# Up-projection by Strassen's seven products on 258-token blocks, its activations through DRAM

## The chip, the core and the metric

The kernel runs on one core of a Trainium2 chip. The metric is device time in microseconds, and lower is better; a run is the time of one launch. TensorE (PE in the profile) multiplies, VectorE (DVE), ScalarE (ACT) and GpSimd (POOL) do the elementwise work, and SyncE (SP) issues the transfers between DRAM and the on-chip memory (SBUF). Products land in PSUM, which TensorE writes and the other engines read.

## The reference

One layer of a hybrid decoder trunk on 1024 prompt tokens and 8 sample tokens (NT = 1032 columns), 1024 features, all float32. The part that the change touches is the MLP with what stands directly ahead of it and behind it:

```python
x = x + concat([o, sg]) @ w_out                                              # 1024 x 1024
x = x + square(relu(rms_norm(x, g_ff) @ w_up)) @ w_down                      # w_up 1024 x 4096, w_down 4096 x 1024
x = x + (p @ w_ple) * sigmoid(rms_norm(x, g_ple) @ w_ple_gate)
y = rms_norm(x, g_final)
```

Ahead of it lie the input projection, a gated delta rule with four heads, and a causal spatial gate.

## The kernel before

Activations lie feature-major: a tile is 128 features by 1032 tokens. A float32 product is made of three TensorE passes: each operand is split into a rounded half (hi, type fp32r) and the rest (lo), and `gemm_steps` issues hi·hi, lo·hi and hi·lo (lines 164 to 166) into one PSUM block. The tokens go in three blocks of 384, 384 and 264 columns, so that one weight tile of 128 x 128 is loaded for each matmul. Weights come in as tiles `st` of 512 KB; ACT rounds them (`whi`, line 133) and DVE subtracts (`wlo`, line 136).

The program is laid out in stages. From 0 to about 521 us the input projection and the two mixing branches are woven together on TensorE. Then the second half of the out-projection runs (`out_half(1)`, about 522 to 567 us): `evo` adds each block to the residual `X1[m]` on DVE (line 1003) and, in the same place, `split_gain` gives the scaled halves `XN[m]` that the MLP reads (lines 139 and 140). The rms factor needn't be known then: the squares' sum `ss` is built on ACT and POOL (lines 1081 to 1086) beside the first MLP products, and since relu squared is homogeneous, the reciprocal mean square `rr` is multiplied into the down-projection's results (`evd`, line 1151).

The MLP runs in eight groups. A group has four up units (128 hidden features each, eight feature tiles deep), whose evacuation `evu` applies relu and square on ACT and makes the halves of h (lines 1137 to 1140) in the tiles RA[8..15], and then four down units that read these h tiles at once and add to `X1` (DVE line 1151, POOL line 1153; in the last group DVE does the add and `split_gain` for the next stage). The hidden activations never leave SBUF. Weights are taken in the order of the list `plan` by `next_w`: `stage` issues the next tile's transfer on SP (line 1050) and `halves` splits it, one unit ahead. TensorE's order is that of the code; the other engines' order is set by a scheduler that takes instructions with high priority (evacuations, weight halves) first. The engines go through their queues strictly in order, and so does SP, where a transfer that waits holds up those behind it.

Behind the MLP stands the gate stage, which neither kernel makes differently.

Of the kernel before, what the change touches and what calls it, by code (L numbers as in the profile page):

```python
# [8 lines left out]
F32 = mybir.dt.float32  # L9
# [7 lines left out]
P = 128  # L17
# [51 lines left out]
def trunk_step_kernel(  # L69
# [49 lines left out]
    dram = ctx.enter_context(pool("dram", 1, DRAM))

# [4 lines left out]

    RA = [act.tile([P, NT], F32R, name=f"ra{i}") for i in range(16)]
# [15 lines left out]
    def load_w(src, hi_eng=S, lo_eng=V, prio=PRI):  # L142
        """src: [128, k, m] view in DRAM, k * m = 1024."""
        a, b = src.shape[1], src.shape[2]
        st = wst.tile([P, 1024], F32, tag="st", name="st")
        hi = wsp.tile([P, 1024], F32R, tag="whi", name="whi")
        lo = wsp.tile([P, 1024], F32R, tag="wlo", name="wlo")
        with tc.high_priority(prio):
            SY.dma_start(st.rearrange("p (a b) -> p a b", a=a), src)
            split(hi[:, :], lo[:, :], st[:, :], hi_eng, lo_eng)  # L150
        return hi.rearrange("p (a b) -> p a b", a=a), lo.rearrange("p (a b) -> p a b", a=a)

    gps = [None]
# [36 lines left out]
    def weave(main):  # L190
        """Put in main's products; between them, what the tasks have ready by then: a task yields
# [1122 lines left out]
```

## Time and profile before

| | us |
|---|---|
| median of three runs | 1438.74 (1437.06 to 1439.82) |
| span of the profiled execution | 1437.0 |
| TensorE matmuls busy | 1383.8 (96%) |
| VectorE busy | 731.3 (51%) |
| ScalarE busy | 499.0 (35%) |
| GpSimd busy | 496.2 (35%) |

The profiled execution shows its span alone; no separate run time of that same execution is given. The span is read as the length of one launch on the core, and the median of the runs lies 1.7 us above it. Busy shares are averages over all stages. Matmuls are shown pipelined: the duration of one is longer than the distance to the next, so costs of TensorE are taken from the distance between starts.

### The profile page before, as it was taken

The numbers are of one execution on the slowest core, as the hardware profiler recorded it, in microseconds if no ns is written. First come the engines' busy times: TensorE is split into PE (matmuls) and PEld (weight loads), VectorE is DVE, ScalarE is ACT, GpSimd is POOL, SyncE is SP. The second block draws the span as 40 slices with busy tenths as digits, with TensorE's granted clock in tenths as the row PEclk, the third lists the DMA queues.
The fourth block names the chain that finished last, engine by engine and source line by source line (L and its number), as shares of the span: only waits on it lengthen the run. The fifth ranks groups of instructions, "written<-read, shape, count | busy, mean of one in ns | idle before, by whom it ended". The sixth has DMA issues, their size and how long they took to land.

```text
span 1437.0 us, 22992 instructions
## 1 busy us (share of the span) xinstructions
PE 1383.8 (96%) x9087; PEld 1358.1 (95%) x9087; DVE 731.3 (51%) x1452; ACT 499.0 (35%) x1056; POOL 496.2 (35%) x590
## 2 busy tenths in 40 slices
PE   6999978999998999999999999999999999998998
PEld 4999977999898999999999999999999999998998
DVE  7746655368847656333433333434333333496336
ACT  6576546432234235312203122131121311344345
POOL 5301987847416215042140321403214032053331
PEclk8999988999999999999999999999999999999999
DMA  7335536465438531111111111111111111111224
GB/s 232 97 87 154 142 78 156 152 177 154 119 83 237 198 120 45 60 44 45 45 46 58 44 45 45 45 48 56 45 45 45 45 48 56 45 44 45 60 59 162
DMA packets 169095, 126.11 MB, mean 88 GB/s; under 512 B 15937, under 2 KB 156428, under 8 KB 168981
## 3 DMA queue, kind: packets, MB, share of 16 engines
q1 hardware_dynamic: 168988, 124.66, 29.0%
q8 instruction: 71, 1.16, 0.3%
q14 instruction: 36, 0.29, 0.1%
HBM read 97.94 MB, written 26.80 MB: 87 GB/s over the span
## 4 chain that ended last, share of the span: by engine, by line
PE 77%; DVE 10%; POOL 4%; ACT 3%; DMA 3%; issue 2%; SPq 0%; DVEq 0%; ACTq 0%; POOLq 0%
PE g L164 23%; PE g L165 23%; PE g L166 23%; POOL xinv L594 2%; POOL it L593 2%; DVE wlo L136 1%; DVE x L1153 1%; DVE ra L136 1%; PE mx L924 1%; PE em L1192 1%; PE em L1191 1%; PE g L376 1%; PE em L1193 1%; DVE ra L140 1%; DVE rlt L211 1%
## 5 line engine op out<-in xcount | busy, mean ns | idle before, releaser
L164 PE MATMUL g<-ra,whi 128*128 128x384 f32 (+1 forms) x2016 | 667.4, 331 | 1.9 <-DVE t L1151 1.0
L165 PE MATMUL g<-ra,wlo 128*128 128x384 f32 (+1 forms) x2016 | 651.7, 323 | 1.3 <-DVE wlo L136 1.3
L166 PE MATMUL g<-ra,whi 128*128 128x384 f32 (+1 forms) x2016 | 650.6, 323 | 0.6 <-POOL ra L341 0.4
L164 PEld LDWEIGHTS g<-ra,whi 128*128 128x128 f32 x2016 | 384.5, 191 | 4.6 <-DVE t L1151 1.3
L165 PEld LDWEIGHTS g<-ra,wlo 128*128 128x128 f32 x2016 | 384.6, 191 | 2.0 <-DVE wlo L136 1.6
L166 PEld LDWEIGHTS g<-ra,whi 128*128 128x128 f32 x2016 | 383.8, 190 | 2.5 <-POOL ra L341 1.3
L1153 POOL TENSOR_TENSOR x<-x,t 128x384 f32<-128x384 f32 x168 | 155.7, 927 | 479.4 <-DVE t L1151 479.0
L133 ACT CAST whi<-st 128x1024 fp32r<-128x1024 f32 x112 | 117.1, 1046 | 311.2 <-PE g L166 309.3
L1151 DVE TENSOR_TENSOR t<-g,rr 128x384 f32<-128x384 f32 (+1 forms) x192 | 98.6, 513 | 177.4 <-PE g L166 177.4
L136 DVE TENSOR_TENSOR wlo<-st,whi 128x1024 fp32r<-128x1024 f32 x111 | 142.0, 1279 | 53.6 <-ACT whi L133 53.6
L164 PE MATMUL g<-rb,whi 128*128 128x384 f32 (+1 forms) x480 | 154.6, 322 | 0.0
L1139 DVE TENSOR_TENSOR q<-t 128x384 f32<-128x384 f32 (+1 forms) x96 | 49.6, 517 | 204.0 <-ACT t L1137 204.0
L166 PE MATMUL g<-rb,whi 128*128 128x384 f32 (+1 forms) x480 | 153.4, 320 | 0.0
L165 PE MATMUL g<-rb,wlo 128*128 128x384 f32 (+1 forms) x480 | 153.2, 319 | 0.0
L1137 ACT ACTIVATE t<-g 128x384 f32<-128x384 f32 (+1 forms) x96 | 44.0, 458 | 248.7 <-PE g L166 248.7
L1086 POOL TENSOR_TENSOR ss<-ss,q 128x384 f32<-128x384 f32 (+1 forms) x62 | 67.3, 1093 | 167.0 <-ACT q L1085 167.0
L593 POOL TENSOR_TENSOR it<-ainv,xinv 32x31 f32<-32x31 f32 (+15 forms) x124 | 76.1, 614 | 44.5 <-DMA ainv<-inv_d 35.1
L166 PEld LDWEIGHTS g<-rb,whi 128*128 128x128 f32 x480 | 90.6, 189 | 0.0
L165 PEld LDWEIGHTS g<-rb,wlo 128*128 128x128 f32 x480 | 90.5, 189 | 0.0
L164 PEld LDWEIGHTS g<-rb,whi 128*128 128x128 f32 x480 | 90.4, 188 | 0.1
L594 POOL TENSOR_TENSOR xinv<-xinv,it 32x31 f32<-32x31 f32 (+15 forms) x124 | 81.1, 654 | 9.6
L1140 DVE TENSOR_TENSOR ra<-q,ra 128x384 fp32r<-128x384 f32 (+1 forms) x96 | 49.4, 515 | 7.0 <-DVE q L1139 0.5
(339 smaller groups left out, 1374.7 us busy)
## 6 DMA issues: line engine op xcount, KB each, us to landing
st<-in_w_up SPq DMA_DIRECT2D x32, 512.0 KB
st<-in_w_down SPq DMA_DIRECT2D x32, 512.0 KB
st<-in_w_in SPq DMA_DIRECT2D x24, 512.0 KB
ck<-ck_d SPq DMA_DIRECT2D x32, 320.0 KB
st<-in_w_ple_gate SPq DMA_DIRECT2D x16, 512.0 KB
x<-xfm_d SPq DMA_DIRECT2D x8, 516.0 KB
xt<-in_x_prompt SPq DMA_DIRECT2D x8, 512.0 KB
s<-in_state_gdn SPq DMA_DIRECT2D x8, 512.0 KB
```

The source lines that it names most:

```text
L133: S.copy(dst_hi, src)
L136: lo_eng.tensor_sub(dst_lo, src, f32(dst_hi))
L164: PE.matmul(ps[:, :w], lhsT=whi[k], rhs=xh, start=(k == 0), stop=False)
L165: PE.matmul(ps[:, :w], lhsT=wlo[k], rhs=xh, start=False, stop=False)
L166: PE.matmul(ps[:, :w], lhsT=whi[k], rhs=xl, start=False, stop=(k == nk - 1))
L593: G.tensor_mul(tv, a, x)
L594: G.tensor_sub(X[:, j + 1 :, :w], X[:, j + 1 :, :w], tv)
L1086: G.tensor_add(ss[:, b], ss[:, b], q[:, :w])
L1139: V.tensor_mul(q[:, :w], t[:, :w], t[:, :w])
L1140: V.tensor_sub(lo[:, o : o + w], q[:, :w], f32(hi[:, o : o + w]))
L1151: V.tensor_mul(t[:, :w], ps[:, :w], rr[:, o : o + w])
L1153: (V if b == 7 else G).tensor_add(xv, xv, t[:, :w])
```

## The change

The MLP is taken apart into two stages. The up-projection is computed by Strassen's scheme in Winograd's form: the 1024 input features are halved into k = 0..3 and k = 4..7 and the 256 output features of a pair of units into two; the input block's and the weight block's quarters are combined by sums, seven products take the place of eight, and sums of the products give the outputs. The tokens are cut into four blocks of 258, and a product multiplies one combination on 258 columns: two token halves t, each with an even and an odd block, are the input's second dimension of the scheme.

For this, the input needs seven combinations per token half, in halves hi and lo. `xform(k, tp)` makes them as soon as `out_half(1)` has finished the feature tiles k and k + 4 on a token half: two ACT scalings (line 1058), three POOL subtractions (lines 1060 to 1062), one ACT rounding (line 1066) and one DVE subtraction (line 1067) of 7 x 258 columns. All eight calls work in one buffer `Q` and write to `FB`, 14 cells of 2064 columns. `up_forms` loads the four quarters of the weights for a pair of units, forms four sums on POOL (lines 1134, 1137, 1140, 1145) and splits seven forms; three forms are kept ahead. `up_stage` runs 16 pairs of 7 products with 2 token halves, 4 feature tiles and 3 passes each on 258 columns, in the PSUM banks A, C, D and E. `hidden` applies relu and square on ACT, a square on POOL and a subtraction on DVE, and stores hi and lo of h to DRAM, `h_d` (line 1201), from two buffers `hs`. The statistics for `rr` are made by `up_rows` beside it (line 1212 is its add on POOL).

The down-projection follows as a separate stage with the blocks and units of before: it loads h from `h_d` into cells of `FB` that the last products have released (`load_h`, line 1296), three groups of four ahead. Its first weight tile lies in a pool `wst2` that takes the space of the up stage's tiles, the second in the older pool `wst`. Weights are split in two forms of 512 columns each instead of one of 1024, everywhere. The core of the diff:

```diff
+HB = NT // 4
+QBLK = [(i * HB, HB) for i in range(4)]
+STEPS = (("P1", 0, "A", True, False), ("P5", 3, "D", True, False), ("P6", 5, "A", False, True), ("P7", 4, "C", True, False),
+         ("P2", 2, "E", True, True), ("P4", 6, "C", False, True), ("P3", 1, "D", False, True))
+FREE = [x[1] for x in STEPS]
+AHEAD = 3
...
-    wsp = ctx.enter_context(pool("wsp", 2))
...
+    wst = ctx.enter_context(pool("wst", 1, side="right"))
+    wsp = ctx.enter_context(pool("wsp", 4, side="right"))
...
+    def form(src, hi_eng=S, lo_eng=V):
+        hi = wsp.tile([P, 512], F32R, tag="whi", name="whi").rearrange("p (a b) -> p a b", a=4)
+        lo = wsp.tile([P, 512], F32R, tag="wlo", name="wlo").rearrange("p (a b) -> p a b", a=4)
+        split(hi, lo, src, hi_eng, lo_eng)
+        return hi, lo
...
+    h_d = dram.tile([32, P, 2, NT], F32, name="h_d")
...
-            RB = [sr.tile([P, NT], F32R, tag=t, bufs=b, name="rb")
-                  for t, b in (("at", 2), ("at", 2), ("sf", 2), ("sf", 2), ("dt", 1), ("kp", 1), ("kt", 1), ("vt", 1))]
-            XN = [(RA[2 * m], RA[2 * m + 1]) if m < 4 else (RB[2 * m - 8], RB[2 * m - 7]) for m in range(KD)]
...
+                sizes = QBLK if half else BLK
...
-                            if half:
-                                split_gain((XN[m][0][:, b], XN[m][1][:, b]), X1[m][:, b], gff[:, m : m + 1])
...
+                    if half == 0:
+                        for j in range(2):
+                            yield from steps(j, range(NB))
+                    else:
+                        for tp in range(2):
+                            for j in range(2):
+                                yield from steps(j, (2 * tp, 2 * tp + 1))
+                            done(m, tp)
...
+            fst = ctx.enter_context(pool("fst"))
+            FB = fst.tile([P, 14, 8 * HB], F32R, name="fb")
+            Q = fst.tile([P, 8, HB], F32, name="q8")
+            def xform(k, tp):
+                t0 = 2 * HB * tp
+                for i in range(2):
+                    S.activation(Q[:, 2 * i : 2 * i + 2, :].rearrange("p a b -> p (a b)"), X1[k + 4 * i][:, t0 : t0 + 2 * HB],
+                                 AF.Copy, scale=gff[:, k + 4 * i : k + 4 * i + 1])
+                G.tensor_sub(Q[:, 4:6, :], Q[:, 0:1, :].to_broadcast([P, 2, HB]), Q[:, 1:3, :])
+                G.tensor_sub(Q[:, 6, :], Q[:, 2, :], Q[:, 4, :])
+                G.tensor_sub(Q[:, 7, :], Q[:, 3, :], Q[:, 6, :])
+                cells = FB[:, 7 * tp : 7 * tp + 7, :]
+                hi = cells[:, :, HB * k : HB * k + HB]
+                lo = cells[:, :, HB * (k + 4) : HB * (k + 5)]
+                S.copy(hi, Q[:, 1:8, :])
+                V.tensor_sub(lo, Q[:, 1:8, :], f32(hi))
+            weave(out_half(1, xform))
...
-        for j in range(4):
-            hi, lo = RA[8 + 2 * j], RA[9 + 2 * j]
-
-            def evu(ps, n, o, w):
-                t = tp.tile([P, BW], F32, tag="t", name="t")
-                q = tp.tile([P, BW], F32, tag="q", name="q")
-                S.activation(t[:, :w], ps[:, :w], AF.Relu)
-                S.activation(hi[:, o : o + w], t[:, :w], AF.Square)
-                V.tensor_mul(q[:, :w], t[:, :w], t[:, :w])
-                V.tensor_sub(lo[:, o : o + w], q[:, :w], f32(hi[:, o : o + w]))
...
+    def up_forms():
+        for p in range(16):
+            with tc.high_priority(PRI):
+                ra = wst.tile([P, 2, 4, P], F32, tag="st", name="ra")
+                rb = [tp.tile([P, 4, P], F32, tag="rb", bufs=4, name="rb") for _ in range(2)]
+                for i in range(2):
+                    SY.dma_start(ra[:, i], up_quarter(2 * p, i))
+                    SY.dma_start(rb[i], up_quarter(2 * p + 1, i))
+            a11, a12 = ra[:, 0], ra[:, 1]
+            a21, a22 = rb
+            yield form(a11)
+            s1 = tp.tile([P, 4, P], F32, tag="sa", bufs=1, name="s1")
+            G.tensor_add(s1, a21, a22)
+            yield form(s1)
+            s2 = tp.tile([P, 4, P], F32, tag="sb", bufs=1, name="s2")
+            G.tensor_sub(s2, s1, a11)
+            yield form(s2)
+            s3 = tp.tile([P, 4, P], F32, tag="sa", bufs=1, name="s3")
+            G.tensor_sub(s3, a21, a11)
+            yield form(s3)
+            yield form(a12)
+            yield form(a22)
+            s4 = tp.tile([P, 4, P], F32, tag="sa", bufs=1, name="s4")
+            G.tensor_sub(s4, a12, s2)
+            yield form(s4)
...
+    def up_stage():
+        forms = up_forms()
+        ahead = [next(forms) for _ in range(AHEAD)]
+        for p in range(16):
+            bank, u1, u2, u3 = {}, {}, {}, {}
+            for name, f, b, first, last in STEPS:
+                wh, wl = ahead.pop(0)
+                w = next(forms, None)
+                if w:
+                    ahead.append(w)
+                for t in range(2):
+                    if first:
+                        bank[b, t] = pu.tile([P, 512], F32, tag=f"{'A' if b == 'E' else b}{t}", name=b)[:, :HB]
+                    ps = bank[b, t]
+                    x = FB[:, 7 * t + f, :].rearrange("p (j k c) -> p j k c", j=2, c=HB)
+                    for k in range(4):
+                        PE.matmul(ps, lhsT=wh[:, k, :], rhs=x[:, 0, k, :], start=(first and k == 0), stop=False, skip_group_check=True)
+                        PE.matmul(ps, lhsT=wl[:, k, :], rhs=x[:, 0, k, :], start=False, stop=False, skip_group_check=True)
+                        PE.matmul(ps, lhsT=wh[:, k, :], rhs=x[:, 1, k, :], start=False, stop=(k == 3), skip_group_check=True)
+                        if k < 3:
+                            yield 3 * HB * 0.000455
+                    q = Q[:, 4 * t : 4 * t + 4, :]
+                    with tc.high_priority(PRI):
+                        if name == "P1":
+                            u1[t] = tp.tile([P, HB], F32, tag="u1", name="u1")
+                            S.copy(u1[t], ps)
+                        elif name == "P6":
+                            u2[t] = tp.tile([P, HB], F32, tag="u2", name="u2")
+                            S.copy(u2[t], ps)
+                        elif name == "P7":
+                            u3[t] = tp.tile([P, HB], F32, tag="u3", name="u3")
+                            V.tensor_add(u3[t], u2[t], ps)
+                            V.tensor_add(q[:, 2], u3[t], bank["D", t])
+                        elif name == "P2":
+                            V.tensor_add(q[:, 1], u1[t], ps)
+                        elif name == "P4":
+                            V.tensor_add(q[:, 3], u2[t], ps)
+                        elif name == "P3":
+                            V.tensor_add(q[:, 0], u2[t], ps)
+                    if name == "P4":
+                        hidden(2 * p + 1, t, q[:, 2:4])
+                    elif name == "P3":
+                        hidden(2 * p, t, q[:, 0:2])
+                    yield 3 * HB * 0.000455
...
+    def hidden(u, t, q):
+        S.activation(q, q, AF.Relu)
+        hs = tp.tile([P, 2, 2 * HB], F32R, tag="hs", name="hs")
+        v = hs.rearrange("p j (a b) -> p j a b", a=2)
+        S.activation(v[:, 0], q, AF.Square)
+        G.tensor_mul(q, q, q)
+        V.tensor_sub(v[:, 1], q, f32(v[:, 0]))
+        SY.dma_start(h_d[u, :, :, 2 * HB * t : 2 * HB * t + 2 * HB], f32(hs))
...
+            ss = tp.tile([P, 264], F32, tag="sq0", bufs=1, name="ssu")
+            S.activation(ss[:, :w], X1[0][:, o : o + w], AF.Square)
+            for m in range(1, KD):
+                q = tp.tile([P, 264], F32, tag="sq1", bufs=1, name="qu")
+                S.activation(q[:, :w], X1[m][:, o : o + w], AF.Square)
+                G.tensor_add(ss[:, :w], ss[:, :w], q[:, :w])
+                yield 5.0
...
+    with tc.manual_schedule(engines={mybir.EngineType.PE}):
+        spawn(up_rows(), 10.0)
+        weave(up_stage())
+        drain()
+    ust.close()
...
+    wst2 = ctx.enter_context(pool("wst2", side="right"))
...
+    cells = [FB[:, 7 * t + f, :] for f in FREE for t in range(2)]
+    def cell(i):
+        v = cells[i].rearrange("p (j c) -> p j c", j=2)
+        return v[:, 0, :], v[:, 1, :]
...
+            st = (wst if n % 2 else wst2).tile([P, 1024], F32, tag="st", name="st")
...
+    xs = [cell((m + 8) % 12) for m in range(KD)]
+    HC = [cell(u % 12) for u in range(32)]
+    def load_h(b):
+        for u in range(4 * b, min(4 * b + 4, 32)):
+            SY.dma_start(f32(cells[u % 12]).rearrange("p (j c) -> p j c", j=2), h_d[u])
+    def down():
+        load_h(0)
+        load_h(1)
+        for b in range(8):
+            load_h(b + 2)
+            hs = HC[4 * b : 4 * b + 4]
+            for m2 in range(4):
+                ws = next_w()
...
```

On POOL, at the start of the up stage, the rows of before are the sums of squares (`ss`) and then the first adds of the down-projection's results:

```order
L1086 TENSOR_TENSOR ss_6389<-ss_6389,q_6445 128x264
L1086 TENSOR_TENSOR ss_6389<-ss_6389,q_6448 128x384
L1086 TENSOR_TENSOR ss_6389<-ss_6389,q_6451 128x384
L1086 TENSOR_TENSOR ss_6389<-ss_6389,q_6454 128x264
L1153 TENSOR_TENSOR x1_5442<-x1_5442,t_6893 128x384
L1153 TENSOR_TENSOR x1_5442<-x1_5442,t_6909 128x384
L1153 TENSOR_TENSOR x1_5442<-x1_5442,t_6925 128x264
```

On POOL of the changed kernel, at the same place, rows from the end of the fifth `xform` into the sixth (`q8` is the buffer `Q`, `s1` to `s4` the weight sums of the first pair, `ssu` the squares' sum):

```order
L1062 TENSOR_TENSOR q8_6085<-q8_6085 128x258
L1212 TENSOR_TENSOR ssu_6789<-ssu_6789,qu_6791 128x256
L1134 TENSOR_TENSOR s1_6652<-rb_6642,rb_6643 128x512
L1212 TENSOR_TENSOR ssu_6789<-ssu_6789,qu_6870 128x256
L1137 TENSOR_TENSOR s2_6658<-s1_6652,ra_6641 128x512
L1140 TENSOR_TENSOR s3_6664<-rb_6642,ra_6641 128x512
L1060 TENSOR_TENSOR q8_6085<-q8_6085 128x516
L1212 TENSOR_TENSOR ssu_6789<-ssu_6789,qu_6952 128x256
L1061 TENSOR_TENSOR q8_6085<-q8_6085 128x258
L1145 TENSOR_TENSOR s4_6762<-ra_6641,s2_6658 128x512
L1212 TENSOR_TENSOR ssu_6789<-ssu_6789,qu_7015 128x256
L1062 TENSOR_TENSOR q8_6085<-q8_6085 128x258
```

Sums of weights and of squares stand ahead of the sixth `xform`'s first subtraction and between its others.

On SP, around the first change from up to down, the rows of before:

```order
L1050 DMA st_6581<-in_w_up 128x8x128
L1117 DMA row_d_99<-row_6474 9x128
L1118 DMA rr_6390<-row_d_99 128x1032
L1050 DMA st_6680<-in_w_down 128x4x256
L1050 DMA st_6779<-in_w_down 128x4x256
L1050 DMA st_6878<-in_w_down 128x4x256
L1050 DMA st_6980<-in_w_down 128x4x256
L1050 DMA st_7082<-in_w_up 128x8x128
```

On SP of the changed kernel, around its one change from up to down (`fb` are the cells that take h, `hs` the stores of h, `st_10984` the second unit's weights and `st_10982` the first unit's):

```order
L1296 DMA fb_6084<-h_d_88 128x2064 x2
L1259 DMA st_10984<-in_w_down 128x4x256
L1296 DMA fb_6084<-h_d_88 128x2064
L1201 DMA h_d_88<-hs_10698 256x1x516
L1296 DMA fb_6084<-h_d_88 128x2064 x3
L1201 DMA h_d_88<-hs_10717 256x1x516
L1296 DMA fb_6084<-h_d_88 128x2064 x5
L1201 DMA h_d_88<-hs_10900 256x1x516
L1201 DMA h_d_88<-hs_10919 256x1x516
L1201 DMA h_d_88<-hs_10938 256x1x516
L1201 DMA h_d_88<-hs_10957 256x1x516
L1259 DMA st_10982<-in_w_down 128x4x256
```

Behind the loads of h now stand four stores and, last, the weights that the first down unit needs.

On ACT, the rows of before at the first change from up to down:

```order
L1138 ACTIVATE ra12_94<-t_6707 128x384
L1137 ACTIVATE t_6738<-g_6713 128x384
L1138 ACTIVATE ra12_94<-t_6738 128x384
L1137 ACTIVATE t_6769<-g_6744 128x264
L133 CAST whi_6775<-st_6680 128x1024
L1138 ACTIVATE ra12_94<-t_6769 128x264
L1137 ACTIVATE t_6806<-g_6781 128x384
```

On ACT of the changed kernel, at its change from up to down:

```order
L142 CAST whi_10822<-s4_10820 128x512
L1195 ACTIVATE q8_6085<-q8_6085 128x516 x3
L1198 ACTIVATE hs_10900<-q8_6085 128x516
L1195 ACTIVATE q8_6085<-q8_6085 128x516
L1198 ACTIVATE hs_10919<-q8_6085 128x516
L1198 ACTIVATE hs_10938<-q8_6085 128x516
L1198 ACTIVATE hs_10957<-q8_6085 128x516
L142 CAST whi_10986<-st_10982 128x512
L142 CAST whi_10990<-st_10982 128x512
L142 CAST whi_11008<-st_10984 128x512
```

The squares that fill the last `hs` buffers now stand ahead of the rounding of the first down weights.

## Rows read from the trace of the kernel before

**Rows 1.** The page's first rows: the span, each engine's busy time:

```profile
span 1437.0 us, 22992 instructions
...
PE 1383.8 (96%) x9087; PEld 1358.1 (95%) x9087; DVE 731.3 (51%) x1452; ACT 499.0 (35%) x1056; POOL 496.2 (35%) x590
```

**Rows 2.** Busy time by engine, 600 to 1250 us (last: granted clock, DMA share, GB/s):

```profile
core 0: us, PE busy (x) PEld busy (x) DVE busy (x) ACT busy (x) POOL busy (x), PEclk, DMA share, GB/s
...
600.00:1250.00 650.00, 650.00 (x4136) 650.00 (x4135) 246.07 (x402) 138.28 (x235) 155.73 (x168) 1.00 0.15 47
```

**Rows 3.** TensorE in order of time (start, duration, line, shape):

```profile
561.10 0.34 PE L164 MATMUL g<-ra,whi 128*128 128x384 f32 x1
...
565.30 0.28 PE L164 MATMUL g<-ra,whi 128*128 128x264 f32 x1
...
577.29 0.28 PE L164 MATMUL g<-ra,whi 128*128 128x264 f32 x1
...
578.75 0.29 PE L164 MATMUL g<-rb,whi 128*128 128x264 f32 x1
```

**Rows 4.** Groups by line and form, 505 to 600 us (count, total, mean):

```profile
L133 ACT CAST whi<-st 128x1024 fp32r<-128x1024 f32 x8 | 8.3, 1041 | 8.3 <-PE g L166 8.3
...
L139 ACT ACTIVATE ra<-x,vec 128x384 fp32r<-128x384 f32 x8 | 4.9, 617 | 8.7 <-DVE x L1003 8.7
...
L139 ACT ACTIVATE ra<-x,vec 128x264 fp32r<-128x264 f32 x4 | 2.1, 513 | 1.4 <-DVE x L1003 1.4
...
L136 DVE TENSOR_TENSOR wlo<-st,whi 128x1024 fp32r<-128x1024 f32 x8 | 9.8, 1228 | 3.2 <-ACT whi L133 3.2
```

**Rows 5.** Groups by line and form, 600 to 1250 us:

```profile
L1153 POOL TENSOR_TENSOR x<-x,t 128x384 f32<-128x384 f32 x112 | 113.6, 1014 | 457.7 <-DVE t L1151 457.7
...
L1153 POOL TENSOR_TENSOR x<-x,t 128x264 f32<-128x264 f32 x56 | 42.2, 753 | 21.7 <-DVE t L1151 21.4 <-DMA st<-in_w_up 0.3
...
L1140 DVE TENSOR_TENSOR ra<-q,ra 128x384 fp32r<-128x384 f32 x59 | 32.9, 558 | 6.5 <-DVE q L1139 0.5
L1138 ACT ACTIVATE ra<-t 128x384 fp32r<-128x384 f32 x59 | 31.0, 526 | 1.9
...
L1138 ACT ACTIVATE ra<-t 128x264 fp32r<-128x264 f32 x29 | 12.3, 425 | 0.0
...
L1140 DVE TENSOR_TENSOR ra<-q,ra 128x264 fp32r<-128x264 f32 x29 | 12.4, 427 | 0.0
```

**Rows 6.** One evacuation in order of time, ACT to DVE:

```profile
600.16 0.49 ACT L1137 ACTIVATE t<-g 128x384 f32<-128x384 f32 x1 [3.16 <-PE g L166]
...
600.69 0.56 DVE L1139 TENSOR_TENSOR q<-t 128x384 f32<-128x384 f32 x1 [2.98 <-ACT t L1137]
```

**Rows 7.** Transfers on the chain that ended last (start, us, what):

```profile
108.94 3.58 DMA at<-rb_d
...
504.13 6.03 DMA st<-in_w_ple
```

**Rows 8.** Three busy stretches of transfers, columns as in rows 2:

```profile
465.00:470.00 5.00, 4.30 (x23) 3.98 (x21) 5.00 (x4) 2.92 (x8) 4.53 (x3) 0.72 1.06 376
15.00:20.00 5.00, 2.63 (x9) 1.69 (x9) 3.56 (x9) 2.59 (x6) 1.21 (x2) 0.72 1.01 391
464.40:467.80 3.40, 3.40 (x18) 3.40 (x17) 3.40 (x6) 2.20 (x8) 2.33 (x2) 0.50 1.06 342
```

**Rows 9.** What SP waited for (total us, times, longest):

```profile
SPq L149 <- DMA st<-in_w_out: 9.7, 3, 4.7
```

**Rows 10.** TensorE behind an idle stretch (brackets: idle before, releaser):

```profile
463.58 0.49 PE L685 MATMUL cb<-st,ck 128*128 128x128 f32 x2 [3.31 <-DVE vn L674]
```

**Rows 11.** A stretch of TensorE at the gate stage, columns as in rows 2:

```profile
1304.10:1310.80 6.70, 6.53 (x26) 6.39 (x27) 4.83 (x17) 0.69 (x2) 1.13 (x2) 0.50 0.26 78
```

**Rows 12.** POOL and DVE in order of time, 456 to 460 us:

```profile
456.62 2.57 POOL L972 TENSOR_TENSOR s<-s,ub 128x1024 f32<-128x1024 f32 x1
...
457.14 2.47 DVE L136 TENSOR_TENSOR ra<-uk,ra 128x384 fp32r<-128x384 f32 x1
```

More of the change, by code (lines that the diff above doesn't have):

```diff
@@ L124, in trunk_step_kernel @@
     G.memset(ones, 1.0)
-    RA = [act.tile([P, NT], F32R, name=f"ra{i}") for i in range(16)]
     def f32(ap):
@@ L1063, in trunk_step_kernel @@
[L1063 to L1086 removed]
+                            V.tensor_add(X1[m + 4 * j][:, b], X1[m + 4 * j][:, b], ps[:, :w])
@@ L1160, in trunk_step_kernel, with up_quarter @@
-    wpl = [(x1p.tile([P, D], F32R, name=f"wpl_h{k}"), x1p.tile([P, D], F32R, name=f"wpl_l{k}")) for k in range(2)]
+    ust = ExitStack()
+    tp = ust.enter_context(pool("ut", 2, side="right"))
+    pu = ust.enter_context(pool("pu", 1, PSUM))
+    pss = ust.enter_context(pool("pssu", 2, PSUM))
+    def up_quarter(u, half):
+        return w_up[0, 512 * half : 512 * half + 512, u * P : u * P + P].rearrange("(k p) m -> p k m", p=P)
+    def up_forms():
[23 more added lines that the diff above has]
+            yield form(s4)
@@ new lines, in stage, with halves @@
+    def stage():
+        n = len(staged)
+        if n < len(plan):
+            src, by_m = plan[n]
+            st = (wst if n % 2 else wst2).tile([P, 1024], F32, tag="st", name="st")
+            v = st.rearrange("p (a b) -> p a b", a=4 if by_m else 8)
+            with tc.high_priority(PRI):
+                SY.dma_start(v, src)
+            staged.append([v[:, :, j * P : j * P + P] if by_m else v[:, 4 * j : 4 * j + 4, :] for j in range(2)])
+    def halves():
+        n = len(ready)
+        if n < len(plan):
+            with tc.high_priority(PRI):
+                ready.append([form(x) for x in staged[n]])
@@ new lines, in trunk_step_kernel, with next_w, add_ss @@
+    stage()
+    stage()
+    halves()
+    cur = [0]
+    def next_w():
+        halves()
+        stage()
+        cur[0] += 1
+        return ready[cur[0] - 1]
+    def add_ss(m, b):
+        if m == 0:
+            S.activation(ss[:, b], X1[m][:, b], AF.Square)
+        else:
+            q = tp.tile([P, BW], F32, tag="q", name="q")
+            w = b.stop - b.start
+            S.activation(q[:, :w], X1[m][:, b], AF.Square)
+            G.tensor_add(ss[:, b], ss[:, b], q[:, :w])
+    xs = [cell((m + 8) % 12) for m in range(KD)]
@@ L1161, in trunk_step_kernel @@
+    with tc.manual_schedule(engines={mybir.EngineType.PE}):
+        weave(down())
+    wpl = [[half[:, :D] for half in cell(12 + k)] for k in range(2)]
     for k in range(2):
@@ L1163, in trunk_step_kernel @@
         SY.dma_start(st, w_ple[0, k * P : (k + 1) * P, :])
-        split(wpl[k][0][:, :], wpl[k][1][:, :], st[:, :], S, V)
-    pp = [(RA[8 + 2 * k], RA[9 + 2 * k]) for k in range(2)]
+        split(wpl[k][0], wpl[k][1], st[:, :], S, V)
+    pp = [cell(4 + k) for k in range(2)]
     pt = []
```

215 lines of the change are left out of this document (92 added, 123 removed).

## The prediction

> **What bounds the kernel now.** The page first: TensorE is busy for 1383.8 of 1437.0 us, every other engine for about half or less [rows 1]. An average hides stages, so the busy times by stretch come next: from 600 to 1250 us, the MLP, matmuls fill 650.00 of 650.00 us at clock 1.00, while DVE has 246, ACT 138 and POOL 156 us [rows 2]. Nothing but fewer or shorter matmuls can shorten that stretch, and any idle TensorE there is added in full. The price of a matmul comes from distances between starts: 24 of 384 columns from 561.10 to 565.30 us, 0.175 us each, and 12 of 264 from 577.29 to 578.75, 0.1217 us [rows 3]. A line through both gives 0.119 us for 258 columns. The groups by line give the other engines' prices [rows 4, 5].
>
> **Up-projection: fewer columns.** Before, 32 units x 8 feature tiles x 3 passes = 768 sets of blocks: 1536 matmuls x 0.175 + 768 x 0.1217 = 362.3 us. After, 16 pairs x 7 products x 2 halves x 4 tiles x 3 passes = 2688 x 0.119 = 319.9 us. The gain is 42.4 us; 35.2 if 258 columns cost as much as 264, 46.2 if the price is proportional to the columns (0.1176). The down and gate stages keep their columns (0), and half 1 of the out-projection, 384 matmuls x 0.119 = 45.7 us against 45.3, costs 0.4. So the question is what the new stage borders cost; before, TensorE had work of the same kind on both sides of every unit, and [rows 2] shows no border at all.
>
> **Prices of the new elementwise work.** Each comes from two forms of the same operation, by a line. ACT square or relu on 516 columns: 0.526 at 384, 0.425 at 264, so 0.64; ACT with gain, 0.617 and 0.513, so 0.73; the rounding of 7 x 258 = 1806 columns from 1.041 at 1024 and the same slope, 1.70. DVE: 0.558 at 384, 1.228 at 1024, so 2.05 at 1806, 0.70 at 516 or 512, 0.42 at 258. POOL: 1.014 and 0.753, so 1.30 at 516, 1.29 at 512, 0.74 at 258 [rows 4, 5]. A hand-over between engines takes 0.04 us (600.16 + 0.49 to 600.69) [rows 6].
>
> **Into the up stage: +33 us.** All eight `xform` calls share one buffer, so each waits for the last one's DVE subtraction. One link: 2 x 0.73 ACT, 1.30 + 0.74 + 0.74 POOL, 1.70 ACT, 2.05 DVE and some hand-overs, 8.2 us. The first can begin when half 1 has done 48 matmuls, 5.7 us into it. Eight links end at 5.7 + 65.6 = 71.3 us, while half 1 ends at 45.7. The queue of POOL adds to it: ahead of the sixth link's first subtraction stand `s1`, `s2` and `s3`, and inside it `s4` and adds of squares. `s1` needs the quarter `rb`, whose space is let go by TensorE's last matmul of half 1, and whose transfer takes about 3.6 us (512 KB alone, 3.58 [rows 7]); so `s1` ends near 45.7 + 0.4 + 3.4 + 1.3 = 50.8, `s3` near 54, and the sixth link, due at POOL at 48.2, loses 6 us there and about 2 more inside; the adds ahead of the seventh cost 1. The eighth ends near 81. TensorE can put the first product's first tiles (some 21 matmuls, 2.5 us) ahead of the last links and then waits: 81.5 - 2.5 - 45.7 = 33 us. Ends: 23 if POOL's extra rows find room (the bare chain), 40 if DVE's long subtractions also wait for POOL (below).
>
> **Inside the up stage: 0.** Per pair TensorE needs 20.0 us. ACT has 7 roundings of 512, 8 relus and squares and 4 copies, 11 us; DVE 7 x 0.70 + 4 x 0.70 + 10 x 0.42 = 11.9; POOL 4 x 1.29 + 4 x 1.30 = 10.4, and 2.3 more while the squares' sum runs. Each is under 20. But they aren't independent: a DVE subtraction of 384 columns that takes 0.558 us elsewhere [rows 5] took 2.47 when it began beside a POOL operation, and ended just after it (456.62 + 2.57 = 459.19 against 459.61) [rows 12]. Counting DVE's eleven subtractions with two SBUF operands (7.7 us) and POOL one after the other, the pair needs 18.1 us, 20.4 with the squares: still TensorE, barely. I take 0, and keep the upper end for a rival. The Trainium skill, page "SBUF — State Buffer", section "SBUF: two separate sides", calls this an exclusive lock: of a GpSimd operation and a DVE operation with two SBUF inputs, the one that starts first keeps the pair of ports, and the other fully blocks; 0.558 against 2.47 us here agrees. By that rule, kept to operations with two SBUF inputs, the sum stays as it is.
>
> **From up to down: +32 us.** Before, weights came one tile ahead and h never left the chip. Now twelve loads of h of 1.057 MB each go out as the last pair frees cells, the first 1.4 us after that pair's start; the pair ends at 20.0. Among and behind them SP has five stores of 0.53 MB and, last, the first unit's weights. Together 12.68 + 2.64 + 0.52 = 15.85 MB. The trace's busiest stretches moved 376 and 391 GB/s at a DMA share of one [rows 8]. I take 385: 41.2 us, from 2.6 us on. SP goes in order, and an issue behind others waits, as the out-projection's weights did behind earlier transfers (up to 4.7 us) [rows 9]. The last two squares on ACT wait for `hs` buffers, thus for stores that lie in that stream (the one of `hs_10919` lands near 44.5); then square 0.64, POOL 1.30, DVE 0.70, an issue 0.4, the weights 3.6, and halves 0.63 + 0.70: 8 us. The first down matmul comes at 52.5 us, 32.5 after the last up matmul; I take 32. Ends: 20 if only the loads are ahead (12.68 MB at 391 GB/s, 35 us, and 5 behind), 44 if the rate is the lowest of the three stretches, 342 [rows 8], with two returns of 3.6 us from stores in line rather than beside the loads. The Trainium skill, page "DMA: Bandwidth & Descriptors", gives about 435 GB/s as the fabric's ceiling and about 358 for HBM with one core's share; by 435 the stall would be 27 us, by 358 it would be 36. The trace's 391 speaks against 358 as a ceiling.
>
> **The clock: +3.4 us.** After an idle of 3.31 us [rows 10] TensorE ran 3.40 us at granted clock 0.50, that is 1.2 instead of 2.4 GHz [rows 8], 1.7 us lost. Two long idles cost 2 x 1.7; a stretch of 6.7 us at 0.50 is there too, at the gate stage [rows 11], so 6.8 is the upper end.
>
> **Other edits.** Weights split in two forms cost ACT 2 x 0.63 against 1.04 and DVE 2 x 0.70 against 1.23 per tile, 0.2 us each on engines with room: 0, within 2 us over the in-projection. The down stage's loads of h, 4.2 MB per group of 45 us beside 2.1 MB of weights, need 140 GB/s: hidden, 0.
>
> **Sum.** 1437.0 - 42.4 + 0.4 + 33 + 0 + 32 + 3.4 = 1463.4 us of span; the median lies 1.7 above the profiled span, so 1465.
>
> **Rivals.**
> (a) The borders cost little: POOL's rows find room (23), and the stores and first weights pass the loads, so that only the last pair's own tail (relu, square, POOL, DVE, store, weights, halves: about 9 us) is left. 1437 - 42.4 + 0.4 + 23 + 9 + 3.4 + 1.7 = 1432, faster. It decides if the first weights land within 9 us of the last up matmul. For it: a transfer of 512 KB alone takes 3.58 us; against it: one in company took 6.03 [rows 7], and SP's order puts them last. Chance 0.08.
> (b) DVE and POOL become the up stage's bound: if all of DVE's queue stands still while POOL runs, since the operations behind a blocked one wait too, a pair needs 11.9 + 10.4 = 22.3 us, and 16 x 2.3 = 37 us come on top: 1502. For it: 2.47 us in [rows 12]; against it: ten of DVE's operations read PSUM and can run beside POOL. It decides from the point where less than 2.3 us per pair overlap. Half of it is likelier than all. Chance 0.15, a third of that beyond my range.
> (c) Only one border is at its low end and the columns are proportional (-46.2): about 1437 + 1.7 - 46.2 + 0.4 + 23 + 20 + 3.4 = 1439, no change to measure. Chance 0.04.
> That fewer columns are run is certain: the built program has 2688 matmuls of 258 columns there.
>
> **How the numbers follow.** The forecast as worked out has 0.73. Low end with both borders at their lower bounds, 1441; high end with both at their upper, the clock at 6.8 and the gain 42.4: 1437 - 42.4 + 0.4 + 40 + 44 + 6.8 + 1.7 = 1488, and 1492 with a part of (b). 0.2%, about what a measurement of this kernel can tell from no change, is 2.9 us. Faster is (a), 0.08; within 0.2% 0.04; slower 0.88.
>
> **What would show it.** In the profile after: matmuls 0.119 us apart in the up stage, 320 us of them; one idle of about 33 us ended by DVE's subtraction of 1806 columns, and one of about 32 ended by halves of `w_down`, whose transfer stands last on SP; a granted clock of 0.5 behind both; no idle between pairs. I am wrong if TensorE's idle at either border is under 10 us, or if idle lies scattered over the up stage with DVE or POOL as releaser.

## The result and the profile after

The changed kernel takes 1479.47 us (1478.17 to 1486.15 in four runs), the kernel before 1438.2 (1437.06 to 1439.82) beside it: a ratio of 1.0291, interval 1.0265 to 1.0317. It is slower by 41 us, the forecast was 27. The page of the profiled execution (span, busy time by engine, then two of the rows in 40 slices) answers to [rows 1]:

```profile
span 1477.2 us, 25006 instructions
...
PE 1352.6 (92%) x9567; PEld 1324.4 (90%) x9567; DVE 857.0 (58%) x1635; ACT 568.0 (38%) x1224; POOL 678.4 (46%) x750
...
PE   6979978989998996599999999379999999998998
...
PEclk9999979999999998699999999779999999999999
```

TensorE has 31 us less to do than in [rows 1] and yet ends 40 later. Two dents stand in its row, at the 17th slice (5) and the 26th (3), with a lower granted clock at both. What TensorE waited for (us in all, times, longest):

```profile
PE g L187 <- ACT whi L142: 33.8, 1, 33.8
PE A L1164 <- ACT fb L1066: 25.5, 3, 20.9
...
PE rbT L553 <- DVE of L723: 7.7, 1, 7.7
...
PE A L1166 <- DVE fb L1067: 4.1, 3, 1.6
```

The first is the border from up to down, the second and the fourth the start of the up stage, each where the prediction had put it. The idle into the up stage is not one but six waits, 29.6 us in all, and 25.5 of them end with ACT's rounding (`fb`, line 1066) rather than with DVE's subtraction. The third was not foreseen; it lies in the mixing stage (below). Busy time in the stretches of the MLP, columns as in [rows 2]:

```profile
core 0: us, PE busy (x) PEld busy (x) DVE busy (x) ACT busy (x) POOL busy (x), PEclk, DMA share, GB/s
...
611.60:617.30 5.70, 5.70 (x26) 5.70 (x27) 0.69 (x1) 0.89 (x2) 0.00 (x0) 0.50 0.33 95
617.30:631.60 14.30, 14.30 (x122) 14.30 (x121) 8.25 (x15) 6.40 (x12) 5.49 (x5) 1.00 0.13 38
631.60:935.50 303.90, 303.68 (x2540) 303.40 (x2539) 202.34 (x316) 156.47 (x304) 162.64 (x137) 1.00 0.49 168
918.10:959.50 41.40, 17.50 (x144) 17.09 (x143) 8.55 (x17) 7.54 (x14) 4.91 (x5) 0.74 1.00 389
935.50:969.60 34.10, 0.33 (x3) 0.12 (x2) 3.31 (x7) 3.78 (x8) 4.37 (x4) 0.54 0.88 346
961.00:969.60 8.60, 0.00 (x0) 0.00 (x0) 1.49 (x4) 1.24 (x3) 1.52 (x2) 0.50 0.72 249
969.60:975.70 6.10, 6.02 (x18) 5.62 (x19) 5.33 (x7) 3.44 (x5) 0.66 (x1) 0.50 0.69 232
```

In the steady stretch 2540 matmuls start in 303.9 us, 0.1196 us apart, at clock 1.00 and with no idle to speak of: the shorter up stage is real, and DVE and POOL do not bound it. From starts of matmuls, the 40.2 us between the two profiled spans come apart like this:

| part | forecast | measured |
|---|---|---|
| all up to the end of half 1 | +0.4 (±2) | +9.2 (575.91 against 566.76) |
| TensorE's idle into the up stage | +33 | +33.2 (575.91 to 611.97, less the 24 matmuls in it at 0.119: six waits, 29.6, and matmuls at the lower clock between them) |
| up matmuls, slow clock behind the idle included | -40.7 | -35.9 |
| border from up to down | +32 | +34.1 (start to start) |
| down stage with its slow clock, gate stage and outputs | +1.7 | -0.4 (what is left) |

The clock's part of these: half of the 5.7 us from 611.6 and of the 6.1 us from 969.6, in which 0.50 was granted, some 3 us each against 1.7 each in the forecast.

The first row of the table is sure to some 2.5 us only: in the profiles of the three runs below whose edits lie at the border and behind it (two groups, first weights, border rebuilt) the first up product starts at 577.67, 574.17 and 572.83 us, here at 575.91.

**The start chain** shows in POOL's rows around the sixth transform, in order of time (start, duration; in brackets the idle before and its releaser):

```profile
578.69 2.44 POOL L1134 TENSOR_TENSOR s<-rb 128x512 f32<-128x512 f32 x1 [1.53 <-DMA rb<-in_w_up]
...
581.77 1.27 POOL L1137 TENSOR_TENSOR s<-s,ra 128x512 f32<-128x512 f32 x1
583.73 1.26 POOL L1140 TENSOR_TENSOR s<-rb,ra 128x512 f32<-128x512 f32 x1 [0.69 <-DVE wlo L145]
584.95 1.63 POOL L1060 TENSOR_TENSOR q<-q 128x516 f32<-128x516 f32 x1
...
588.37 1.26 POOL L1145 TENSOR_TENSOR s<-ra,s 128x512 f32<-128x512 f32 x1
```

The weight sum waits for the quarter that could only be loaded behind half 1, and the transform's first subtraction stands behind three sums. The last DVE subtractions of the transforms, which close each link:

```profile
569.25 2.03 DVE L1067 TENSOR_TENSOR fb<-q,fb 128x1806 fp32r<-128x1806 f32 x1
577.97 2.04 DVE L1067 TENSOR_TENSOR fb<-q,fb 128x1806 fp32r<-128x1806 f32 x1 [1.42 <-ACT fb L1066]
592.67 2.04 DVE L1067 TENSOR_TENSOR fb<-q,fb 128x1806 fp32r<-128x1806 f32 x1 [5.53 <-ACT fb L1066]
...
609.49 2.04 DVE L1067 TENSOR_TENSOR fb<-q,fb 128x1806 fp32r<-128x1806 f32 x1 [5.93 <-ACT fb L1066]
```

A link takes 8.0 to 9.7 us (8.2 forecast), the sixth 14.7.

**The border** in SP's rows of the transfers it issued (duration includes its waits):

```profile
923.66 5.04 SPq L1296 DMA_DIRECT2D fb<-h_d  x3
...
931.58 8.01 SPq L1296 DMA_DIRECT2D fb<-h_d  x5
941.75 22.43 SPq L1201 DMA_DIRECT2D h_d<-hs  x4
964.24 0.60 SPq L1259 DMA_DIRECT2D st<-in_w_down  x1
```

and in ACT's:

```profile
959.53 0.63 ACT L1198 ACTIVATE hs<-q 128x516 fp32r<-128x516 f32 x1 [13.23 <-DMA h_d<-hs]
960.98 0.63 ACT L1198 ACTIVATE hs<-q 128x516 fp32r<-128x516 f32 x1 [0.82 <-DMA h_d<-hs]
968.97 2.18 ACT L142 CAST whi<-st 128x512 fp32r<-128x512 f32 x4 [7.36 <-DMA st<-in_w_down]
```

Loads of h, then stores that hold up the squares, then the weights that end the wait, in the order that the built program had. The last pair begins at 915.06; the last square is let go 45.9 us later (the prediction has the store that it waits for land near 44.5), and from there to the first down matmul, at 969.64, it takes 8.7 us (8 forecast).

### The profile page after: what moved, and what is told of

It is laid out like the page before. It is cut to its first block, busy times and chain, and to the rows that moved or that the text cites. A ratio compares the mean times of both kernels' runs of the same rounds, so it can differ in the third digit from the quotient of the medians.

```text
span 1477.2 us, 25006 instructions
## 1 busy us (share of the span) xinstructions
PE 1352.6 (92%) x9567; PEld 1324.4 (90%) x9567; DVE 857.0 (58%) x1635; ACT 568.0 (38%) x1224; POOL 678.4 (46%) x750
## 4 chain that ended last, share of the span: by engine, by line
PE 73%; DVE 8%; POOL 7%; DMA 5%; ACT 3%; issue 2%; SPq 1%; DVEq 0%; POOLq 0%; ACTq 0%
PE g L187 15%; PE g L189 15%; PE g L188 15%; POOL xinv L619 3%; POOL it L618 3%; DMA h_d<-hs 3%; PE D L1165 2%; PE D L1166 2%; PE D L1164 2%; PE A L1166 2%; PE C L1164 2%; PE C L1165 2%; PE C L1166 2%; PE A L1164 2%; PE A L1165 2%
## 5 line engine op out<-in xcount | busy, mean ns | idle before, releaser
L187 PE MATMUL g<-fb,whi 128*128 128x384 f32 (+1 forms) x960 | 310.1, 323 | 34.3 <-ACT whi L142 33.8
L189 PE MATMUL g<-fb,whi 128*128 128x384 f32 (+1 forms) x960 | 308.4, 321 | 0.0
L188 PE MATMUL g<-fb,wlo 128*128 128x384 f32 (+1 forms) x960 | 308.3, 321 | 0.0
L187 PE MATMUL g<-ra,whi 128*128 128x384 f32 (+2 forms) x800 | 274.0, 342 | 0.7 <-ACT ra L365 0.7
L189 PE MATMUL g<-ra,whi 128*128 128x384 f32 (+2 forms) x800 | 257.6, 322 | 0.8 <-POOL ra L366 0.4
L188 PE MATMUL g<-ra,wlo 128*128 128x384 f32 (+2 forms) x800 | 256.7, 321 | 0.0
L187 PEld LDWEIGHTS g<-fb,whi 128*128 128x128 f32 x960 | 181.8, 189 | 35.1 <-ACT whi L142 34.0
L145 DVE TENSOR_TENSOR wlo<-st,whi 128x512 fp32r<-128x512 f32 x158 | 149.5, 948 | 64.7 <-ACT whi L142 59.1
L188 PEld LDWEIGHTS g<-fb,wlo 128*128 128x128 f32 x960 | 181.7, 189 | 0.4 <-DVE wlo L145 0.4
L189 PEld LDWEIGHTS g<-fb,whi 128*128 128x128 f32 x960 | 181.6, 189 | 0.0
L187 PEld LDWEIGHTS g<-ra,whi 128*128 128x128 f32 x800 | 155.6, 194 | 2.8 <-ACT ra L365 1.1
L189 PEld LDWEIGHTS g<-ra,whi 128*128 128x128 f32 x800 | 154.8, 193 | 2.5 <-POOL ra L366 1.6
L188 PEld LDWEIGHTS g<-ra,wlo 128*128 128x128 f32 x800 | 155.8, 195 | 0.7 <-DVE wlo L145 0.3
L1164 PE MATMUL A<-fb,whi 128*128 128x258 f32 x256 | 73.5, 287 | 25.5 <-ACT fb L1066 25.5
L1166 PE MATMUL A<-fb,whi 128*128 128x258 f32 x256 | 73.7, 288 | 4.1 <-DVE fb L1067 4.1
```

The costliest lines, as they stand in the source:

```text
L145: lo_eng.tensor_sub(dst_lo, src, f32(dst_hi))
L187: PE.matmul(ps[:, :w], lhsT=whi[k], rhs=xh, start=(k == 0), stop=False)
L188: PE.matmul(ps[:, :w], lhsT=wlo[k], rhs=xh, start=False, stop=False)
L189: PE.matmul(ps[:, :w], lhsT=whi[k], rhs=xl, start=False, stop=(k == nk - 1))
L1164: PE.matmul(ps, lhsT=wh[:, k, :], rhs=x[:, 0, k, :], start=(first and k == 0), stop=False, skip_group_check=True)
L1166: PE.matmul(ps, lhsT=wh[:, k, :], rhs=x[:, 1, k, :], start=False, stop=(k == 3), skip_group_check=True)
```

## Experiments

The theory is the prediction's, with two serial places; what it had not foreseen is the 9 us that have been lost by the end of half 1.

**Splitting in two forms, alone.** On the kernel before:

```diff
-    wsp = ctx.enter_context(pool("wsp", 2))
+    wsp = ctx.enter_context(pool("wsp", 4))
...
-            split(hi[:, :], lo[:, :], st[:, :], hi_eng, lo_eng)
...
+        for j in range(2):
+            hi = wsp.tile([P, 512], F32R, tag="whi", name="whi")
+            lo = wsp.tile([P, 512], F32R, tag="wlo", name="wlo")
+            split(hi[:, :], lo[:, :], st[:, 512 * j : 512 * j + 512], hi_eng, lo_eng)
```

> The kernel before with one edit: each weight tile is split in two forms of 512 columns with tiles of their own (four of each in the pool) instead of one of 1024. In the changed kernel the stages ahead of the out-projection's half 1 took 9 us longer (half 1 begins near 530.8 us instead of 521.8). Theory: the forms alone do that, since in the mixing stage ACT and DVE sit on TensorE's path and each tile now puts two instructions in their queues: half 1 begins near 531, 1447 us in all. Rival: the forms cost nothing (0.2 us per tile on engines with room) and the 9 us come from the other layout of the pools and the order that follows from it: half 1 begins near 522, 1438 us.

1450.0 us against 1439.54, ratio 1.0073 (1.0056 to 1.009). The forms alone cost as much as was missing (9.2). One place where they do it: TensorE's transpose `rbT` of the first head waits for

```profile
PE rbT L538 <- DVE of L708: 7.7, 1, 7.7
```

as it does in the changed kernel (7.7), and not in the kernel before, where it waits 1.9 us for `rkb`. DVE's rows in this kernel, in order of time:

```profile
101.14 0.18 DVE L524 TENSOR_SCALAR ssf<-ssf 128x16 f32<-128x16 f32 x1
101.22 1.28 DVE L477 SCALAR_TENSOR_TENSOR kq<-pre,vec,kq 128x1024 f32<-128x1024 f32 x1
...
102.53 1.28 DVE L477 SCALAR_TENSOR_TENSOR kq<-pre,vec,kq 128x1024 f32<-128x1024 f32 x1
...
105.93 0.16 DVE L530 TENSOR_TENSOR rkb<-rkq,beta 128x8 f32<-128x8 f32 x1
```

and in the kernel before:

```profile
98.64 0.17 DVE L514 TENSOR_SCALAR ssf<-ssf 128x16 f32<-128x16 f32 x1 [0.16 <-ACT sq L511]
...
101.23 0.16 DVE L520 TENSOR_TENSOR rkb<-rkq,beta 128x8 f32<-128x8 f32 x1
```

The chain of small operations from `ssf` to `rkb` took 2.7 us; now it takes 4.9 and begins 2.5 later, since convolution steps of 1.28 us (two among these rows, one just ahead, at 99.85) have moved in front of it and into it; in the kernel before the three stand behind it, from 104.70 on. TensorE stands for 7.7 us meanwhile, and `rbT` starts at 106.2 instead of 101.6. Here the price of the forms is not their 0.2 us each but another order of DVE's queue, which the scheduler built from the changed pieces. TensorE is 4.6 us late here, of 10.5 in all; where the rest is lost was not followed, and that it too comes from the order is likely but not shown.

**Whole splits again, on the changed kernel.** One ACT and one DVE instruction per tile of 1024, `wsp` with two tiles; the up stage's forms take halves of such tiles.

```diff
-            return [form(x, lo_eng=lo_eng) for x in parts]
+            return form1(st, by_col if by_m else by_row, lo_eng=lo_eng)
...
+    def form1(st, pick, hi_eng=S, lo_eng=V):
+        hi = wsp.tile([P, 1024], F32R, tag="whi", name="whi")
+        lo = wsp.tile([P, 1024], F32R, tag="wlo", name="wlo")
+        split(hi[:, :], lo[:, :], st[:, :], hi_eng, lo_eng)
+        return [(pick(hi, j), pick(lo, j)) for j in range(2)]
```

> The changed kernel, but a weight tile of 1024 columns is again split by one ACT and one DVE instruction, as in the kernel before (the up stage's seven forms take halves of such tiles). Theory, from the forms tried on the kernel before, which took 10.5 us more: half 1 of the out-projection begins near 521 us instead of 530.8, 1469 us in all, the two idles at the borders as they were (33 and 34 us). Rival (in the changed kernel the order of the mixing stage differs for other reasons too): half 1 still begins after 528, 1477. A risk: tiles shared by two forms come free later, which would show as short idles inside the up stage.

1472.67 us, ratio to the kernel before 1.0238 (1.021 to 1.0266); the first up product starts 7.3 us earlier and `rbT` waits 1.9 us again. The border grows by 2 us; the first unit's weights are now rounded whole before any product, which is 0.4 of it (1.04 us against 0.61), and the rest was not followed:

```profile
PE g L203 <- ACT whi L142: 35.7, 1, 35.7
```

So 7 of the 9 us are undone by that part alone, a little less than the 10 us that were expected; the other 2 are within the spread named above.

**h two groups ahead.**

```diff
-    HC = [cell(u % 12) for u in range(32)]
+    HC = [cell(u % 8) for u in range(32)]
...
-        load_h(1)
         for b in range(8):
-            load_h(b + 2)
+            load_h(b + 1)
```

> The changed kernel, but h is loaded two groups ahead instead of three: eight loads of 1.057 MB instead of twelve stand on SP ahead of the last stores and the first down weights. Theory (the stream of transfers sets the border): four loads less are 4.2 MB, at 385 GB/s 11 us; TensorE's idle at the border falls from 33.8 to about 23, 1468 us in all. Rival (what counts is the chain of returns of the last four hs buffers, store, landing, square, which no load lengthens): 34 us stay, 1479.

```profile
PE g L187 <- ACT whi L142: 24.7, 1, 24.7
```

1467.69 us (two runs, as in the experiments from here to the rebuilt border). Four loads less take 9.1 us of idle, where 11 were expected from 4.2 MB. The transfers in the stream, not the returns of the buffers alone, set the border.

**The first unit's weights early.**

```diff
-            st = (wst if n % 2 else wst2).tile([P, 1024], F32, tag="st", name="st")
+            st = (wst2 if n % 2 else wst).tile([P, 1024], F32, tag="st", name="st")
```

> The changed kernel, but the first down unit's weights take the older tile (wst) and the second unit's the one in the up stage's space, so that the first unit's transfer stands fourth on SP and its halves ahead of the last squares on ACT. If the late weights alone were the cause, the idle of 33.8 us would go, 1446 us. Theory: the evacuation tile t and DVE's queue stand behind the same hs buffers, so TensorE fills its four PSUM blocks (7.8 us) and then waits until DVE has done the last hs subtraction, 28 us behind the last up matmul, and once more for the second unit's weights: about 24 us of idle are left, 1469.

1464.3 us; TensorE's waits and DVE's rows:

```profile
PE g L187 <- DVE t L1311: 22.4, 2, 22.0
```

```profile
961.89 0.69 DVE L1200 TENSOR_TENSOR hs<-q,hs 128x516 fp32r<-128x516 f32 x1 [0.94 <-POOL q L1199]
962.50 1.35 DVE L1311 TENSOR_TENSOR t<-g,rr 128x384 f32<-128x384 f32 x3
```

The wait has moved: the first four blocks run at once, and the evacuation then stands behind the last `hs` subtraction on DVE. Weights that are late are what ended the wait in the profile, but without them 22.0 of the 33.8 us stay: the `hs` buffers, on which DVE's queue stands, are a second cause beside them.

**The transform's subtractions on DVE.**

```diff
-                G.tensor_sub(Q[:, 4:6, :], Q[:, 0:1, :].to_broadcast([P, 2, HB]), Q[:, 1:3, :])
-                G.tensor_sub(Q[:, 6, :], Q[:, 2, :], Q[:, 4, :])
-                G.tensor_sub(Q[:, 7, :], Q[:, 3, :], Q[:, 6, :])
+                V.tensor_sub(Q[:, 4:6, :], Q[:, 0:1, :].to_broadcast([P, 2, HB]), Q[:, 1:3, :])
+                V.tensor_sub(Q[:, 6, :], Q[:, 2, :], Q[:, 4, :])
+                V.tensor_sub(Q[:, 7, :], Q[:, 3, :], Q[:, 6, :])
```

> The changed kernel, but the three subtractions of each input transform are done by DVE instead of POOL. Theory (one chain through a single buffer, lengthened by POOL's weight sums that stand in its queue): a link falls from 8.2 to 7.0 us and POOL's other rows are out of its way; eight links end at 5.7 + 56 = 62 us of half 1, TensorE's idle at the start of the up stage falls from some 32 us to 14 to 18, 1462 to 1465 us in all. Rival (POOL's other rows cost nothing, the chain alone counts): only 8 x 1.2 = 10 us are gained, 1469. Rival (the wait is for the weights' quarters and sums, not for the transform): nothing changes, 1479.

1468.55 us: the waits for the transforms are 22.0 us (19.4 and 2.6) instead of 29.6. That is the time of the rival that counted the chain alone (1469), but not for its reason. By that rival every link would be 1.2 us shorter; the links from the second on take 7.8 to 8.7 us, not 7.0, except the seventh (10.5), and the gain is at the sixth, which POOL's sums no longer stand in front of: 8.2 us instead of 14.7.

```profile
574.28 2.03 DVE L1067 TENSOR_TENSOR fb<-q,fb 128x1806 fp32r<-128x1806 f32 x1
...
578.45 1.37 DVE L1061 TENSOR_TENSOR q<-q 128x258 f32<-128x258 f32 x1
...
582.50 2.04 DVE L1067 TENSOR_TENSOR fb<-q,fb 128x1806 fp32r<-128x1806 f32 x1
...
588.51 1.32 DVE L1060 TENSOR_TENSOR q<-q 128x516 f32<-128x516 f32 x1 [1.16 <-ACT q L1058]
```

POOL's sums still take part, from the other side: DVE's subtractions of the sixth and seventh transform run beside them and take 1.37 us where 0.42 is the price elsewhere, and 1.32 where 0.69 is; and the splits of the weight sums now stand in DVE's queue among them (L145, one of 1.75 us, two in 2.88). My value of 14 to 18 us was too good.

**Transforms in halves.** Two half-transforms of 129 columns, each with half of `Q`.

```diff
+            Qh = Q.rearrange("p a b -> p (a b)").rearrange("p (j a b) -> p j a b", j=2, a=8)
...
+                for h in range(2):
+                    q = Qh[:, h]
```

> The changed kernel, but each input transform is done in two halves of 129 columns, each with half of the buffer Q, so that two are under way at once; the same work on the same engines. Theory (a serial chain through one buffer): half a link takes some 5 us, two overlap, and the transforms keep up with half 1; only those of the last feature tiles come late, and POOL's weight sums, which wait for the quarters that come in behind half 1, still stand ahead of the last one's subtractions. TensorE's idle at the start of the up stage falls from some 32 to about 12 us, 1459 us in all. Rival (the engines' work, not the one buffer, sets it, as smaller instructions cost more in sum): the idle stays over 25 us, 1475 or more.

```profile
PE A L1168 <- ACT fb L1070: 10.3, 2, 7.9
...
PE A L1170 <- DVE fb L1071: 1.5, 2, 1.1
```

1459.48 us: the same work on the same engines, and 11.8 us of waits instead of 29.6. So the single buffer was the cause of most of the wait, as said. What is left is the wait for the last transforms, whose subtractions still share POOL's queue with the weight sums.

**The border rebuilt.** Two groups ahead, the first weights in `wst`, the last pair's `hs` in freed cells, `t` in `Q`.

```diff
+        if u >= 30:
+            c = 4 * HB * (31 - u)
+            hs = FB[:, 7 * t + FREE[4], c : c + 4 * HB].rearrange("p (j b) -> p j b", j=2)
...
+        else:
+            hs = tp.tile([P, 2, 2 * HB], F32R, tag="hs", name="hs")
...
+                            c = BW * (slot[0] % 5)
+                            t = Q.rearrange("p a b -> p (a b)")[:, c : c + BW]
```

> The changed kernel with only the change from up to down rebuilt: h loaded two groups ahead instead of three, the first unit's weights in the older tile, the last pair's hs halves put in freed cells of FB instead of the two hs buffers, and the evacuations' t in the buffer Q, so that neither waits for stores. Theory: with no evacuation or square behind the stream of transfers, the first down matmul comes within 1 us of the last up matmul; the second unit's weights, behind eight loads and the stores, cost some 5 us; so 33.8 becomes about 5, the lost clock behind it (3.3 us) comes back too, 1448 us in all. Rival (h itself isn't there: the loads are limited by the rate, so that the products wait for cells): 15 us or more are left, released by a transfer of h, 1460.

1453.19 us, where 1448 was expected; 3 of the 26 us gained lie ahead of the up stage, within the spread named above. The first down matmul comes at once; the second unit's weights cost 10.6 us, not 5:

```profile
PE g L187 <- ACT whi L142: 10.6, 1, 10.6
```

```profile
925.00:943.00 18.00, 17.81 (x126) 17.60 (x126) 12.28 (x25) 5.88 (x10) 9.21 (x9) 1.00 1.02 408
943.00:954.00 11.00, 0.48 (x4) 0.27 (x3) 0.43 (x1) 0.56 (x2) 1.44 (x2) 0.71 1.04 361
```

The transfers are saturated through the whole border (DMA share over one, 408 and 361 GB/s, columns as above): so what remains is, as far as these rows show, the stream itself.

**All three together** (whole splits, halves with the last transforms' subtractions on DVE, the rebuilt border):

> All three together on the changed kernel: whole splits of weight tiles, transforms in two halves (those of the last feature tiles with their subtractions on DVE, out of the way of POOL's weight sums), and the rebuilt change from up to down. Theory: each cost is of its own place, so the gains add: 1479.5 - 9.5 (splits) - 25 (start of the up stage, idle near 7 us) - 29 - 5 (clock) gives 1411 us, under the kernel before by some 27. Rival (they aren't independent: what waits less at the borders meets a bound of DVE and POOL inside the up stage): idle is scattered over the pairs, 1425 or more.

1425.58 us, ratio to the kernel before 0.9919 (0.9894 to 0.9944): 0.8% under the kernel before, and the interval excludes no change. Its span, its up stage (columns as above) and its waits:

```profile
span 1422.0 us, 24770 instructions
...
579.10:902.70 323.60, 323.18 (x2683) 322.52 (x2684) 201.84 (x333) 162.28 (x323) 174.44 (x147) 0.99 0.48 160
```

```profile
PE g L203 <- ACT whi L142: 7.0, 2, 6.2
PE A L1184 <- ACT fb L1086: 5.6, 2, 4.0
PE g L204 <- DVE wlo L145: 4.2, 3, 2.4
...
PE A L1186 <- DVE fb L1087: 3.0, 2, 1.7
```

The time is the one that the rival gave (1425 or more), but not by its mechanism: the up stage takes 323.6 us as against 323.9 in the changed kernel, with no idle scattered over its pairs. It is 14 us short of the 1411 expected mainly because the border keeps some 11 us, where 5 were expected, and the start 8.6 instead of 7, with slow clock behind both.

## Why the prediction was right, and where it was off

The direction and the places were right, and the time lies 14 us above the forecast: 8.8 us are lost by the end of half 1, where the edits were put at nothing (7 of them are shown to be theirs), 4.8 from the up matmuls and 2.1 from the border, and the rest of the kernel gives 2.1 back. Rival (a) fell, since neither border was cheap.

- **The up matmuls** (-42.4): the distance of 0.119 us, drawn from two widths, was measured as 0.1196 over 2540 of them. The step holds. Net, 35.9 us came back; 2.9 of the missing went to the clock, 1.6 to the 0.0006 us more per matmul, and what the other 2 went to was not followed.
- **Into the up stage** (+33, measured 33.2): the chain and the place where POOL's queue lengthens it (the sixth link) are as told; halving the links took 17.8 us of the 29.6 away, and moving the subtractions off POOL took the sixth link's excess away. That the value is right to a quarter of a us is partly luck: most links were nearer to 9 than 8.2, the sixth lost 6 us where 8 were counted and the seventh none where 1 was, and 3.6 us of the 33.2 are slow matmuls between the waits and not idle. What would show it was told wrongly in part: not one idle that DVE's subtraction ends, but six waits, most of their time ended by ACT's rounding, since a product's first pass reads only the rounded half.
- **From up to down** (+32, measured 34.1): the mechanism and its order are as told. With fewer loads, with early weights and with the rebuilt border 24.7, 22.0 and 10.6 us were left where 23, 24 and 5 were expected. The rate of 385 GB/s holds for the stretch that it was meant for: 389 at a DMA share of 1.00 from the first loads to the landing of the store that the last square but one waits for. The 346 GB/s over TensorE's idle are lower because the returns behind that landing leave transfers standing (249 GB/s at 0.72).
- **Inside the up stage** (0): right. Rival (b) fell: 0.2 us of idle in 303.9, though single DVE subtractions took 1.13 and 1.47 us instead of 0.7 beside POOL. One reading in the working is wrong: with the squares' sum it counts 20.4 us for DVE and POOL, which is above TensorE's 20.0 and not "still TensorE". The rows show no wait of that kind.
- **The clock** (+3.4): some 5.9; TensorE was granted 0.50 for 5.7 and 6.1 us behind the two idles, against 3.40 in the one row that I had taken it from. The row at the gate stage (6.7 us), taken for the upper end, was the nearer one.
- **Other edits** (0, within 2 us): this is the step that failed. It counted what two forms cost in engine time, 0.2 us per tile, and not what they do to the order on engines that stand in TensorE's path in the mixing stage. Measured: 10.5 us in the kernel before, 7 in the changed one; the changed order is shown at one place, where TensorE is 4.6 us late. The built program's rows of DVE around the first head might have shown it before any run.
- **Two slips beside the forecast**: the low end of 1441 leaves out the 1.7 us between span and median (1443 with them), and rival (c) speaks of one border at its low end where its sum takes both there (23 and 20).

## What to carry to other kernels

A change that only saves matmuls moves the question to its borders: write down, for the first and the last unit of the new stage, each single buffer and each transfer in the queue, and add up the chain; here both chains came out within some 2 us of the measured time. Splitting one instruction into two, where a scheduler sets the order, is not priced by its engine time: compare the order of the engines wherever they stand in the way of the bounding one. A wait that the profile puts down to its last releaser may have a second, parallel cause just behind it, which may show only when the first is taken away.

## What the runs showed of the hardware

POOL is held up by DVE as DVE is by POOL: the weight sum of 512 columns took 2.44 us when it began beside DVE's subtraction of 1806 columns (2.04 us), and 1.27 alone. The exclusive lock of the Trainium skill, page "SBUF — State Buffer", section "SBUF: two separate sides", reads this way in both directions, and these rows agree. With loads and stores of 1.06 and 0.53 MB in line the chip moved 408 GB/s over 18 us in the run with the rebuilt border, more than in any stretch of [rows 8]. And TensorE was granted 0.50 for 6.1 us behind the idle of 33.8 us and for 5.7 us behind the last of the six waits, a longer slow stretch than the 3.40 us behind the 3.31 us of [rows 10].
